# Hybrid diffusion step on one core: the adaLN sums of a feed-forward stage go behind its opening border, and each norm's reciprocal root takes one GpSimd step instead of two

## The chip, the cores and the metric

One Trainium2 chip, one core. The metric is the device time of one launch in microseconds; lower is better. Engines are called by the profile's names: PE (TensorE), DVE (VectorE), ACT (ScalarE), POOL (GpSimd) and SP (SyncE, which only issues transfers here).

## The reference, cut to what matters

Two layers of a hybrid backbone work on 128 context tokens and 256 latent tokens of width 1024, that is on three tiles of 128 tokens (t = 0 and 1 latent, t = 2 context). Each layer is a SwiGLU feed-forward step, a token mixing step and a second feed-forward step. Around each of them stands a norm, with shift, scale and gate from the conditioning vector (adaLN):

```python
def rms_norm(x, g):
    y = x * lax.rsqrt(jnp.mean(x * x, axis=-1, keepdims=True) + EPS)
    return y * g

m = jax.nn.silu(cond) @ p["w_ada"][l] + p["b_ada"][l]      # shift, scale, gate of 3 sub-layers
def pre(y, i):  return rms_norm(y, p["norm_pre"][l, i]) * (1.0 + scale[:, :, i]) + shift[:, :, i]
def post(y, i): return gate[:, :, i] * rms_norm(y, p["norm_post"][l, i])

x = x + 0.5 * post(swiglu(pre(x, 0), ...), 0)
x = x + post(token_mix(pre(x, 1), ...), 1)
x = x + 0.5 * post(swiglu(pre(x, 2), ...), 2)
```

Inside the mixing step there are further norms over heads of 64 (queries and keys of one attention group, the output of the other) and a layer norm.

## The kernel before

Weights stream in as 128x1024 fp32 pieces (`st`, queued on SP) and each is split into a rounded part and a remainder: ACT casts the first half of the tile `wu` (L167), DVE subtracts for the second (L168). Activations are split the same way (`split_pair`, L478 on ACT and L479 on DVE), and every product is three matmuls on PE (L556 to L558, L562 to L564, L590 to L592).

The stages run in the order ffn(0,0), mix(0), ffn(0,2), ffn(1,0), mix(1), ffn(1,2). Each ends in `rows_out`, the output product `ps_o`, whose last part runs token tile by token tile; behind the last matmul of a tile stand `post` (the sum of squares on ACT, `yg` on DVE, the reciprocal root on POOL, the new `x` on DVE) and `pre` of the next stage (squares of `x`, reciprocal root, `xn` on DVE, eight transposes `ps_t` on PE, `hf` on DVE and ACT, the split `h` on ACT and DVE). So there are five borders between stages: B1 (ffn(0,0) to mix(0)), B2 (mix(0) to ffn(0,2)), B3 (ffn(0,2) to ffn(1,0)), B4 (ffn(1,0) to mix(1)) and B5 (mix(1) to ffn(1,2)). At a border PE works on `ps_o` of the remaining tiles and then on the first projections of the next stage, `ps_j` in a mixing stage (24 matmuls of 512 columns for a token tile) and `ps_gu` in a feed-forward stage (also 24 for a tile), tile by tile.

A reciprocal root takes two steps on POOL: `ms` adds the two half sums and EPS (L489), `rstd` raises to the power -0.5 (L493). Inside the mixing stages L470 and L474 do the same for the head norms and the layer norm.

The adaLN vectors of coming sub-layers are summed inside the feed-forward stages: `Ada.step` multiplies a 128x1024 piece of `w_ada` (`ast`, queued on SP among the `st`) into two accumulators `acc` on DVE (L284 for the first piece, L288 for the others), and PE adds up the partitions when all eight are in (`ps_ada`, L300). The function `more` calls it a few times for every group of output columns.

The kernel's text is not in the order in which the engines work. A scheduler goes over the whole program, and by its own estimate of durations it decides for each engine the order of its queue; the engines then work through their queues in that order, and each instruction waits for its inputs by semaphores.

Of the kernel before, what the change touches and what calls it, by code (L numbers as in the profile page):

```python
# [2 lines left out]

# [1 line left out]

# [22 lines left out]
EPS = 1e-6  # L28
# [158 lines left out]
def kernel(ctx: ExitStack, tc: tile.TileContext, a: dict):  # L187
    nc = tc.nc
    PS = bass.MemoryType.PSUM

    cp = ctx.enter_context(tc.tile_pool(name="cp", bufs=1))
# [6 lines left out]
    sm = ctx.enter_context(tc.tile_pool(name="sm", bufs=4))  # L198
# [24 lines left out]
    x = []  # L223
    for t in range(NT):
        xt = xp.tile([P, D], F32, name=f"x{t}")
        src = a["x_sample"][0, t * P : (t + 1) * P, :] if t < 2 else a["x_prompt"][0]
        x.append((xt, src))

    mhalf = cp.tile([P, 8], F32, name="mhalf")
    nc.gpsimd.memset(mhalf, -0.5)  # L230
    ones = cp.tile([P, 32], F32, name="ones")
    nc.gpsimd.memset(ones, 1.0)
    sink = cp.tile([P, D], BF16, name="sink")
# [5 lines left out]
        out=sc,  # L239
        in_=scol.rearrange("p (i k) -> p k i", i=2).unsqueeze(2).to_broadcast([P, KC, 16, 2]),  # L240
# [148 lines left out]
    x = [t for t, _ in x]  # L389
# [75 lines left out]
            )  # L465


    def rstd_of(ss, n, width):
        ms = sm.tile([P, 8], F32, tag="ms", name=nm("ms"))
        nc.gpsimd.tensor_scalar(  # L470
            out=ms[:, 0:n], in0=ss, scalar1=1.0 / width, scalar2=EPS, op0=ALU.mult, op1=ALU.add
        )
        r = sm.tile([P, 8], F32, tag="rstd", name=nm("rstd"))
        nc.gpsimd.tensor_tensor(out=r[:, 0:n], in0=ms[:, 0:n], in1=mhalf[:, 0:n], op=ALU.pow)  # L474
        return r

    def split_pair(dst, sl, src):
        nc.scalar.copy(out=dst[:, 0, :, sl], in_=src)  # L478
        nc.vector.tensor_tensor(  # L479
            out=dst[:, 1, :, sl], in0=src, in1=dst[:, 0, :, sl].bitcast(F32), op=ALU.subtract  # L480
        )

    def new_pairs(s):
        return [hp.tile([P, 2, 2, TOK], F32R, tag="hc", name=nm(s)) for _ in range(4)]

    def rstd_two(ss):

        ms = sm.tile([P, 8], F32, tag="ms", name=nm("ms"))
        nc.gpsimd.tensor_scalar(  # L489
            out=ms[:, 0:1], in0=ss[:, 0:1], scalar1=ss[:, 1:2], scalar2=EPS, op0=ALU.add, op1=ALU.add  # L490
        )
        r = sm.tile([P, 8], F32, tag="rstd", name=nm("rstd"))
        nc.gpsimd.tensor_tensor(out=r[:, 0:1], in0=ms[:, 0:1], in1=mhalf[:, 0:1], op=ALU.pow)  # L493
        return r

    def pre_norm(t, xn):
        ss = sm.tile([P, 2], F32, tag="ss", name=nm("ss"))
        for hf in range(2):
            hsl = slice(hf * 512, (hf + 1) * 512)
            nc.scalar.activation(  # L500
                out=sink[:, hsl], in_=x[t][:, hsl], func=AF.Square, scale=D ** -0.5,
                accum_out=ss[:, hf : hf + 1],
            )
        r = rstd_two(ss)
        nc.vector.tensor_scalar(out=xn, in0=x[t], scalar1=r[:, 0:1], scalar2=None, op0=ALU.mult)

    def pre_half(l, i, t, hT, xn, half):
        A, B = mods[(l, i)][half]
        cond = 1 if t == 2 else 0
        sl = slice(t * P, (t + 1) * P)  # L510
        pt = mbank(nm("ps_t"))
        hf = tp.tile([P, 4, P], F32, tag="t2k", name=nm("hf"), bufs=4)
        for q in range(4):
            k = 4 * half + q
            nc.tensor.transpose(pt[:, q * P : (q + 1) * P], xn[:, k * P : (k + 1) * P], ident)
        for q in range(4):
            src = pt[:, q * P : (q + 1) * P]
            sa, sb = A[:, q, cond : cond + 1], B[:, q, cond : cond + 1]
            if q < MOD_DVE[half]:
                nc.vector.tensor_scalar(  # L520
                    out=hf[:, q, :], in0=src, scalar1=sa, scalar2=sb, op0=ALU.mult, op1=ALU.add
                )
            else:
                nc.scalar.activation(out=hf[:, q, :], in_=src, func=AF.Identity, scale=sa, bias=sb)
        for pr in range(2):
            split_pair(hT[2 * half + pr], sl, hf[:, 2 * pr : 2 * pr + 2, :])

    def pre(l, i, t, hT):
        xn = tp.tile([P, D], F32, tag="t4k", name=nm("xn"))
# [4 lines left out]
    def post(l, i, t, y):  # L534
        cond = 1 if t == 2 else 0
        G = gates[(l, i)][cond]
        ss = sm.tile([P, 2], F32, tag="ss", name=nm("ss"))
        yg = tp.tile([P, D], F32, tag="t4k", name=nm("yg"))
        for hf in range(2):
            hsl = slice(hf * 512, (hf + 1) * 512)  # L540
            nc.scalar.activation(
                out=sink[:, hsl], in_=y[hf], func=AF.Square, scale=D ** -0.5, accum_out=ss[:, hf : hf + 1]
            )
            nc.vector.tensor_tensor(out=yg[:, hsl], in0=y[hf], in1=G[:, hsl], op=ALU.mult)
        r = rstd_two(ss)
# [71 lines left out]
    def ffn(l, i, h, adas, nxt, first=None):  # L617
# [27 lines left out]
        with tc.tile_pool(name=nm("fp"), bufs=1) as fp:  # L645
# [3 lines left out]
            for t in range(NT):  # L649
# [71 lines left out]
    def mix(l, h, nxt):  # L721
        with tc.tile_pool(name=nm("mp"), bufs=1) as mp:
# [108 lines left out]
            def d_rows(t, ps):  # L831
# [3 lines left out]
                if t == 2:  # L835
# [4 lines left out]
                nc.vector.tensor_reduce(  # L840
                    out=ss[:, 0:6], in_=sq[:, 0:384].rearrange("p (h d) -> p h d", h=6), axis=AX.X, op=ALU.add
                )
                r = rstd_of(ss[:, 0:6], 6, 64)
                dn = mp.tile([P, 512], F32, tag="qk", name=nm("dn"), bufs=2)
                dv = dn[:, 0:384].rearrange("p (h d) -> p h d", h=6)
                nc.vector.tensor_tensor(
# [3 lines left out]
                    op=ALU.mult,  # L850
# [115 lines left out]
            def diff_unit(t, hd, box):  # L966
# [28 lines left out]
                def third():  # L995
# [129 lines left out]
            def norm_fill(t):  # L1125
# [172 lines left out]
```

## Time and profile before

| | before |
|---|---|
| device time, median of 3 runs | 1543.93 us (1543.18 to 1545.84) |
| the profiled execution: its time, its span | 1548.72 us, 1546.9 us |
| PE busy | 1492.0 us, 96% of the span |
| DVE busy | 1048.2 us, 68% |
| ACT busy | 635.4 us, 41% |
| POOL busy | 131.4 us, 8% |
| granted PE clock, mean | 0.993 of full speed |
| HBM | 256.36 MB read, 167 GB/s |

Busy time is the time in which an engine has an instruction in work. PE is busy nearly all the time, so a change in the time has to show in PE's idle time or in its clock.

### The profile page before, as it was taken

The numbers are of one execution on the slowest core, as the hardware profiler recorded it, in microseconds if no ns is written. First come the engines' busy times: TensorE is split into PE (matmuls) and PEld (weight loads), VectorE is DVE, ScalarE is ACT, GpSimd is POOL, SyncE is SP. The second block draws the span as 40 slices with busy tenths as digits, with TensorE's granted clock in tenths as the row PEclk, the third lists the DMA queues.
The fourth block names the chain that finished last, engine by engine and source line by source line (L and its number), as shares of the span: only waits on it lengthen the run. The fifth ranks groups of instructions, "written<-read, shape, count | busy, mean of one in ns | idle before, by whom it ended". The sixth has DMA issues, their size and how long they took to land. (4 is left out here: it accounts for less than half of the span.)

```text
span 1546.9 us, 20700 instructions
## 1 busy us (share of the span) xinstructions
PE 1492.0 (96%) x7924; PEld 1312.3 (85%) x7924; DVE 1048.2 (68%) x1454; ACT 635.4 (41%) x1103; POOL 131.4 (8%) x234
## 2 busy tenths in 40 slices
PE   5999999999999999999999999999999999999997
PEld 3799997777887899998879999887778879999885
DVE  3688889768887846677694666984798785334432
ACT  3442333273575633333263332334545763323331
POOL 1101000021011201000021000001200120000000
PEclk9999999999999999999999999999999999999999
DMA  8678667732224646566655566773322345344431
GB/s 318 231 235 274 228 223 242 242 109 97 69 69 150 204 133 203 201 214 195 197 166 182 183 196 202 234 237 100 124 74 91 108 146 168 123 136 141 134 108 41
DMA packets 73619, 260.13 MB, mean 168 GB/s; under 512 B 9728, under 2 KB 9856, under 8 KB 73520
## 3 DMA queue, kind: packets, MB, share of 16 engines
q1 hardware_dynamic: 68112, 246.32, 48.8%
q0 software_dynamic: 4976, 11.70, 2.8%
q8 instruction: 62, 1.02, 0.3%
q10 hardware_dynamic: 432, 0.79, 0.1%
q14 instruction: 37, 0.30, 0.1%
HBM read 256.36 MB, written 2.41 MB: 167 GB/s over the span
## 5 line engine op out<-in xcount | busy, mean ns | idle before, releaser
L168 DVE TENSOR_TENSOR wu<-st,wu 128x1024 fp32r<-128x1024 f32 x322 | 390.6, 1218 | 258.9 <-ACT wu L167 258.3
L167 ACT CAST wu<-st 128x1024 fp32r<-128x1024 f32 x322 | 337.1, 1052 | 536.2 <-PE ps_f L564 266.4
L562 PE MATMUL ps_f<-h,wu 128*128 128x384 f32 x1248 | 419.0, 336 | 0.0
L564 PE MATMUL ps_f<-h,wu 128*128 128x384 f32 x1248 | 417.1, 334 | 0.0
L563 PE MATMUL ps_f<-h,wu 128*128 128x384 f32 x1248 | 417.1, 334 | 0.0
L288 DVE SCALAR_TENSOR_TENSOR acc<-ast,sc,acc 128x1024 f32<-128x1024 f32 x224 | 279.6, 1281 | 35.0 <-DMA ast<-w_ada 34.6
L562 PEld LDWEIGHTS ps_f<-h,wu 128*128 128x128 f32 x1248 | 234.2, 188 | 7.5 <-issue 7.5
L563 PEld LDWEIGHTS ps_f<-h,wu 128*128 128x128 f32 x1248 | 234.3, 188 | 0.0
L564 PEld LDWEIGHTS ps_f<-h,wu 128*128 128x128 f32 x1248 | 234.2, 188 | 0.0
L590 PE MATMUL ps_o<-wu,hid_s 128*128 128x512 f32 x528 | 207.7, 393 | 0.0
L592 PE MATMUL ps_o<-wu,hid_s 128*128 128x512 f32 x528 | 206.3, 391 | 0.0
L591 PE MATMUL ps_o<-wu,hid_s 128*128 128x512 f32 x528 | 206.2, 391 | 0.0
L590 PEld LDWEIGHTS ps_o<-wu,hid_s 128*128 128x128 f32 x528 | 99.5, 188 | 26.0 <-issue 5.0
L592 PEld LDWEIGHTS ps_o<-wu,hid_s 128*128 128x128 f32 x528 | 99.5, 188 | 21.0
L591 PEld LDWEIGHTS ps_o<-wu,hid_s 128*128 128x128 f32 x528 | 99.6, 189 | 20.3
L702 ACT ACTIVATE sg<-ps_f 128x384 f32<-128x384 f32 x78 | 38.0, 487 | 114.1 <-PE ps_f L564 111.0
L556 PE MATMUL ps_j<-wu,h 128*128 128x512 f32 (+1 forms) x192 | 72.8, 379 | 0.0
L558 PE MATMUL ps_j<-wu,h 128*128 128x512 f32 (+1 forms) x192 | 70.5, 367 | 1.1 <-DVE h L479 1.1
L703 DVE TENSOR_TENSOR hid<-sg,ps_f 128x384 f32<-128x384 f32 x78 | 42.9, 550 | 40.4 <-PE ps_f L564 40.3
L557 PE MATMUL ps_j<-wu,h 128*128 128x512 f32 (+1 forms) x192 | 69.8, 363 | 0.0
L825 DVE SCALAR_TENSOR_TENSOR cacc<-upad,late,cacc 128x399 f32<-128x399 f32 x120 | 69.3, 628 | 0.0
L331 POOL DMA_DIRECT2D gd<-grow x24 | 11.8, 497 | 660.3 <-DVE grow L323 660.3
(234 smaller groups left out, 1698.1 us busy)
## 6 DMA issues: line engine op xcount, KB each, us to landing
st<-ws SPq DMA_DIRECT2D x320, 512.0 KB, 4.3
ast<-w_ada SPq DMA_DIRECT2D x128, 512.0 KB, 4.4
a<-ada SPq DMA_DIRECT2D x16, 512.0 KB, 10.2
G<-gd POOLq DMA_DIRECT2D x12, 512.0 KB, 4.2
brow<-b_ada POOLq DMA_DIRECT2D x24, 64.0 KB, 6.7
prow<-norm_post POOLq DMA_DIRECT2D x24, 64.0 KB, 6.9
x<-x_sample SPq DMA_DIRECT2D x2, 512.0 KB, 5.6
x<-x_prompt SPq DMA_DIRECT2D x1, 512.0 KB, 10.6
```

Of the source, the lines that this page charges most:

```text
L167: nc.scalar.copy(out=u[:, 0, :], in_=x)
L168: nc.vector.tensor_tensor(out=u[:, 1, :], in0=x, in1=u[:, 0, :].bitcast(F32), op=ALU.subtract)
L288: nc.vector.scalar_tensor_tensor(out=self.acc[c], in0=w, scalar=s1, in1=self.acc[c], op0=ALU.mult, op1=ALU.add)
L556: nc.tensor.matmul(out, lhsT=hk(h, k, 0, tsl), rhs=wh, start=start, stop=False)
L557: nc.tensor.matmul(out, lhsT=hk(h, k, 0, tsl), rhs=wl, start=False, stop=False)
L558: nc.tensor.matmul(out, lhsT=hk(h, k, 1, tsl), rhs=wh, start=False, stop=stop)
L562: nc.tensor.matmul(out, lhsT=wh, rhs=hk(h, k, 0, sl), start=start, stop=False)
L563: nc.tensor.matmul(out, lhsT=wh, rhs=hk(h, k, 1, sl), start=False, stop=False)
L564: nc.tensor.matmul(out, lhsT=wl, rhs=hk(h, k, 0, sl), start=False, stop=stop)
L590: nc.tensor.matmul(out, lhsT=pr[:, 0, s, tsl], rhs=u[:, 0, hsl], start=(q == 0), stop=False)
L591: nc.tensor.matmul(out, lhsT=pr[:, 0, s, tsl], rhs=u[:, 1, hsl], start=False, stop=False)
L592: nc.tensor.matmul(out, lhsT=pr[:, 1, s, tsl], rhs=u[:, 0, hsl], start=False, stop=(q == n - 1))
```

## The change

Three edits. First, `split_pair` returns its DVE instruction, `pre_half` keeps the last one in `border[0]`, and in a feed-forward stage every `Ada.step` is issued behind it: the scheduler has to queue each `acc` of the stage behind the last split of the border that opens the stage. (For ffn(0,0) there is no such border, and `edge` is None.) Second, the sums of squares of `post` and `pre`: each `Square` is followed on ACT by an `Identity` on 128x1 that adds EPS to the first half sum and, for the second half, the first result; POOL keeps only the power. Third, `ms` of the norms inside the mixing stage moves from POOL to DVE (`guarded`).

```diff
-    def rstd_of(ss, n, width):
+    def rstd_of(ms, n):
+        r = sm.tile([P, 8], F32, tag="rstd", name=nm("rstd"))
+        nc.gpsimd.tensor_tensor(out=r[:, 0:n], in0=ms, in1=mhalf[:, 0:n], op=ALU.pow)
+        return r
+
+    def guarded(ss, n, width):
         ms = sm.tile([P, 8], F32, tag="ms", name=nm("ms"))
-        nc.gpsimd.tensor_scalar(
+        nc.vector.tensor_scalar(
             out=ms[:, 0:n], in0=ss, scalar1=1.0 / width, scalar2=EPS, op0=ALU.mult, op1=ALU.add
         )
...
+        return rstd_of(ms[:, 0:n], n)
+
+    def half_square(half, src, ss):
+
+        nc.scalar.activation(
+            out=sink[:, 0:512], in_=src, func=AF.Square, scale=D ** -0.5, accum_out=ss[:, half : half + 1]
+        )
+        nc.scalar.activation(
+            out=ss[:, 2 + half : 3 + half], in_=ss[:, half : half + 1], func=AF.Identity,
+            bias=(ss[:, 2:3] if half else guard),
+        )
+
+    border = [None]
 
     def split_pair(dst, sl, src):
         nc.scalar.copy(out=dst[:, 0, :, sl], in_=src)
-        nc.vector.tensor_tensor(
+        return nc.vector.tensor_tensor(
...
-    def rstd_two(ss):
-
-        ms = sm.tile([P, 8], F32, tag="ms", name=nm("ms"))
-        nc.gpsimd.tensor_scalar(
-            out=ms[:, 0:1], in0=ss[:, 0:1], scalar1=ss[:, 1:2], scalar2=EPS, op0=ALU.add, op1=ALU.add
-        )
...
     def pre_norm(t, xn):
...
+            half_square(hf, x[t][:, hf * 512 : (hf + 1) * 512], ss)
+        r = rstd_of(ss[:, 3:4], 1)
...
-            split_pair(hT[2 * half + pr], sl, hf[:, 2 * pr : 2 * pr + 2, :])
+            border[0] = split_pair(hT[2 * half + pr], sl, hf[:, 2 * pr : 2 * pr + 2, :]).ins
...
             done, turns = [], []
+            edge = border[0]
...
-                    last = f.step(fp)
+                    with tc.issue_after(edge) if edge is not None else nullcontext():
+                        last = f.step(fp)
...
-                r = rstd_of(ss[:, 0:6], 6, 64)
+                r = guarded(ss[:, 0:6], 6, 64)
```

(`post` calls `half_square` in place of its `Square` as `pre_norm` does; the three norms of the mixing stage call `guarded`.)

All of this moves instructions in the queues, also where nothing was edited. Three places follow, with the rows of before first and those of the changed kernel second; line numbers of the changed kernel are 2 to 17 higher.

PE at B1, around the transposes of the second token tile. `ps_j_2843` and `ps_j_2845` are the projection of the first tile, `ps_j_2871` and `ps_j_2873` that of the second, `xn_2691` and `xn_2693` the second tile's normalised rows.

```order
L557 MATMUL ps_j_2843<-wu_2823,h_2561 128x512
L515 MATMUL ps_t_2700<-early,xn_2691 128x128 x4
L515 MATMUL ps_t_2714<-early,xn_2691 128x128 x4
L558 MATMUL ps_j_2843<-wu_2823,h_2561 128x512
L556 MATMUL ps_j_2843<-wu_2823,h_2561 128x512
L557 MATMUL ps_j_2843<-wu_2823,h_2561 128x512
...
L558 MATMUL ps_j_2843<-wu_2828,h_2562 128x512
L556 MATMUL ps_j_2871<-wu_2531,h_2559 128x512
```

```order
L558 MATMUL ps_j_2845<-wu_2830,h_2564 128x512
L559 MATMUL ps_j_2845<-wu_2830,h_2564 128x512
L518 MATMUL ps_t_2702<-early,xn_2693 128x128 x4
L518 MATMUL ps_t_2716<-early,xn_2693 128x128 x4
L557 MATMUL ps_j_2873<-wu_2533,h_2561 128x512
L558 MATMUL ps_j_2873<-wu_2533,h_2561 128x512
```

Before, 14 of the first tile's 24 matmuls stand ahead of the second tile's transposes and 10 behind them. Now all 24 stand ahead, and right behind the transposes comes a matmul that needs their result. The same has happened at the other borders: at B2, B3 and B5 the first tile had 6 or 7 of its 24 `ps_gu` ahead of those transposes and now has 24; ahead of the third tile's transposes stand now 24 `ps_j` of the second tile (before 15) at B1 and B4, and 42 `ps_gu` (before 29) at the others.

DVE at B1, second tile: `yg`, the new `x`, weight remainders `wu`, and `xn`.

```order
L544 TENSOR_TENSOR yg_2680<-ps_o_1987,G_1980 128x512
L548 SCALAR_TENSOR_TENSOR x_91<-yg_2680,rstd_2687,x_91 128x512 x2
L168 TENSOR_TENSOR wu_2823<-st_2478,wu_2823 128x1024
L168 TENSOR_TENSOR wu_2828<-st_2501,wu_2828 128x1024
L505 TENSOR_SCALAR xn_2691<-x_91,rstd_2697 128x1024
L544 TENSOR_TENSOR yg_2753<-ps_o_1988,G_1982 128x512
L544 TENSOR_TENSOR yg_2753<-ps_o_1989,G_1982 128x512
L520 TENSOR_SCALAR hf_2701<-ps_t_2700,A_1833,B_1834 128x128 x2
```

```order
L545 TENSOR_TENSOR yg_2682<-ps_o_1989,G_1982 128x512
L168 TENSOR_TENSOR wu_2825<-st_2480,wu_2825 128x1024
L168 TENSOR_TENSOR wu_2830<-st_2503,wu_2830 128x1024
L549 SCALAR_TENSOR_TENSOR x_91<-yg_2682,rstd_2689,x_91 128x512 x2
L168 TENSOR_TENSOR wu_2835<-st_2536,wu_2835 128x1024
L168 TENSOR_TENSOR wu_2840<-st_2559,wu_2840 128x1024
L508 TENSOR_SCALAR xn_2693<-x_91,rstd_2699 128x1024
L545 TENSOR_TENSOR yg_2755<-ps_o_1990,G_1984 128x512
L545 TENSOR_TENSOR yg_2755<-ps_o_1991,G_1984 128x512
L523 TENSOR_SCALAR hf_2703<-ps_t_2702,A_1835,B_1836 128x128 x2
```

Two `wu` now stand ahead of `x` that stood behind it, and two more have come in between `x` and `xn`; `x` and `xn` themselves are as before.

DVE at the opening of B2, first tile: `acc` are adaLN sums, `ast` their pieces of `w_ada`.

```order
L288 SCALAR_TENSOR_TENSOR acc_4650<-ast_4730,sc,acc_4650 128x1024
L544 TENSOR_TENSOR yg_4333<-ps_o_4202,G_4197 128x512
L548 SCALAR_TENSOR_TENSOR x_90<-yg_4333,rstd_4340,x_90 128x512 x2
L288 SCALAR_TENSOR_TENSOR acc_4651<-ast_4730,sc,acc_4651 128x1024
L505 TENSOR_SCALAR xn_4344<-x_90,rstd_4350 128x1024
L544 TENSOR_TENSOR yg_4406<-ps_o_4203,G_4197 128x512
L288 SCALAR_TENSOR_TENSOR acc_4650<-ast_4799,sc,acc_4650 128x1024
```

```order
L545 TENSOR_TENSOR yg_4335<-ps_o_4203,G_4199 128x512
L545 TENSOR_TENSOR yg_4335<-ps_o_4204,G_4199 128x512
L549 SCALAR_TENSOR_TENSOR x_90<-yg_4335,rstd_4342,x_90 128x512 x2
L508 TENSOR_SCALAR xn_4346<-x_90,rstd_4352 128x1024
L545 TENSOR_TENSOR yg_4408<-ps_o_4205,G_4199 128x512
L523 TENSOR_SCALAR hf_4356<-ps_t_4355,A_2572,B_2573 128x128 x2
```

The three `acc` of these rows have gone, and so have those that stood ahead of and behind them; they come now behind the last split `h` of the third tile. In the same way they have left B3 and B5.

## Rows read from the trace of the kernel before

**Rows 1.** The waits of PE over the whole span: what PE waited for, us in total, times, the longest in us.

```profile
PE ps_t L515 <- DVE xn L505: 14.9, 14, 2.7
PE ps_dT L873 <- DVE dr L757: 3.4, 2, 1.7
```

**Rows 2.** The timeline of PE at the first border (B1), from 316 to 341 us: start in us, duration in us, engine, line, operation, tiles, shape, count, and in brackets the idle time before it and what ended it.

```profile
317.68 1.06 PE L515 MATMUL ps_t<-early,xn 128*128 128x128 f32 x8 [1.28 <-DVE xn L505]
318.50 0.47 PE L590 MATMUL ps_o<-wu,hid_s 128*128 128x512 f32 x1
318.82 0.39 PE L591 MATMUL ps_o<-wu,hid_s 128*128 128x512 f32 x1
319.05 0.40 PE L592 MATMUL ps_o<-wu,hid_s 128*128 128x512 f32 x1
...
329.13 1.09 PE L515 MATMUL ps_t<-early,xn 128*128 128x128 f32 x8 [1.05 <-DVE xn L505]
...
333.76 0.50 PE L558 MATMUL ps_j<-wu,h 128*128 128x512 f32 x1 [0.56 <-DVE h L479]
...
337.51 1.09 PE L515 MATMUL ps_t<-early,xn 128*128 128x128 f32 x8 [0.50 <-DVE xn L505]
```

**Rows 3.** The waits of PE again, of one border each: first B4 (1061 to 1100 us, two rows), then B2 (496 to 526 us, three), B3 (783 to 814 us, three) and B5 (1248 to 1279 us, its first row; its other two read as those of B2).

```profile
PE ps_t L515 <- DVE xn L505: 2.8, 3, 1.3
PE ps_j L558 <- DVE h L479: 0.6, 1, 0.6
...
PE ps_t L515 <- DVE xn L505: 3.8, 3, 2.7
PE ps_gu L557 <- DVE wu L168: 0.6, 1, 0.6
PE ps_gu L556 <- ACT h L478: 0.3, 1, 0.3
...
PE ps_t L515 <- DVE xn L505: 2.6, 2, 2.0
PE ps_gu L556 <- ACT h L478: 0.6, 1, 0.6
PE ps_gu L557 <- DVE wu L168: 0.2, 1, 0.2
...
PE ps_t L515 <- DVE xn L505: 2.8, 3, 1.7
```

**Rows 4.** The timeline of DVE around the second token tile of B1 (columns as in Rows 2).

```profile
322.82 0.69 DVE L544 TENSOR_TENSOR yg<-ps_o,G 128x512 f32<-128x512 f32 x1
323.87 1.42 DVE L548 SCALAR_TENSOR_TENSOR x<-yg,rstd,x 128x512 f32<-128x512 f32 x2 [0.36 <-POOL rstd L493]
325.21 2.35 DVE L168 TENSOR_TENSOR wu<-st,wu 128x1024 fp32r<-128x1024 f32 x2
328.32 0.75 DVE L505 TENSOR_SCALAR xn<-x,rstd 128x1024 f32<-128x1024 f32 x1 [0.77 <-POOL rstd L493]
```

**Rows 5.** The timeline of ACT at B1: the first tile (two rows), the second (one), the third (one).

```profile
318.79 1.51 ACT L524 ACTIVATE hf<-ps_t,B,A 128x128 f32<-128x128 f32 x4 [2.51 <-PE ps_t L515]
320.17 0.72 ACT L478 CAST h<-hf 128x256 fp32r<-128x256 f32 x2
...
322.91 2.01 ACT L167 CAST wu<-st 128x1024 fp32r<-128x1024 f32 x2
...
334.94 1.28 ACT L806 ACT_TABLE_LOAD   x1
```

**Rows 6.** The timeline of POOL at B1, second tile.

```profile
326.26 1.38 POOL L489 TENSOR_SCALAR ms<-ss 128x1 f32<-128x1 f32 x1 [1.83 <-ACT sink L500]
327.73 0.56 POOL L493 TENSOR_TENSOR rstd<-ms,mhalf 128x1 f32<-128x1 f32 x1
```

**Rows 7.** The timeline at the other borders: DVE and POOL at B2, then POOL at B3 and at B5.

```profile
491.00 1.28 DVE L288 SCALAR_TENSOR_TENSOR acc<-ast,sc,acc 128x1024 f32<-128x1024 f32 x1 [2.06 <-DMA ast<-w_ada]
...
490.19 0.57 POOL L493 TENSOR_TENSOR rstd<-ms,mhalf 128x1 f32<-128x1 f32 x1
...
777.56 1.82 POOL L489 TENSOR_SCALAR ms<-ss 128x1 f32<-128x1 f32 x1 [9.79 <-ACT sink L541]
...
1243.64 1.53 POOL L493 TENSOR_TENSOR rstd<-ms,mhalf 128x1 f32<-128x1 f32 x1
```

**Rows 8.** Groups of instructions by line with shapes kept apart: busy us, mean ns of one | idle time before them and what ended it.

```profile
L452 ACT ACTIVATE lam<-lam 128x4 f32<-128x4 f32 x1 | 0.2, 207 | 3.4 <-DVE lam L451 3.4
L524 ACT ACTIVATE hf<-ps_t,B,A 128x128 f32<-128x128 f32 x90 | 35.4, 463 | 23.5 <-PE ps_t L515 23.2
L489 POOL TENSOR_SCALAR ms<-ss 128x1 f32<-128x1 f32 x36 | 23.7, 658 | 255.1 <-ACT sink L541 191.7 <-ACT sink L500 62.8
L470 POOL TENSOR_SCALAR ms<-ss 128x6 f32<-128x6 f32 x6 | 4.2, 708 | 50.9 <-DVE ss L840 50.9
L168 DVE TENSOR_TENSOR wu<-st,wu 128x1024 fp32r<-128x1024 f32 x320 | 389.3, 1222 | 258.9 <-ACT wu L167 258.3
```

**Rows 9.** Busy time by engine, 785.7 to 789.0 us, just behind the first transposes of B3: start and end, us, then busy us of each engine (instructions); the third figure from the end is the granted clock as a share of full speed.

```profile
785.70:789.00 3.30, 3.30 (x10) 2.52 (x9) 3.30 (x8) 3.24 (x11) 0.62 (x1) 0.50 0.02 5
```

**Rows 10.** The start: timeline of PE from 0 to 20 us.

```profile
14.12 2.27 PE L404 MATMUL ps_first<-a,sc 128*32 128x256 f32 x16 [14.12 <-DMA a<-ada]
...
19.27 0.38 PE L1236 MATMUL ps_t<-early,xn 128*128 128x128 f32 x2
```

More of the change, by code (lines that the diff above doesn't have):

```diff
@@ L1 @@
 import math
-from contextlib import ExitStack
+from contextlib import ExitStack, nullcontext
 import numpy as np
@@ L230 @@
     nc.gpsimd.memset(mhalf, -0.5)
+    guard = cp.tile([P, 1], F32, name="guard")
+    nc.gpsimd.memset(guard, EPS)
     ones = cp.tile([P, 32], F32, name="ones")
@@ L465, in lam_setup @@
             )
-    def rstd_of(ss, n, width):
+    def rstd_of(ms, n):
[3 more added lines that the diff above has]
+    def guarded(ss, n, width):
         ms = sm.tile([P, 8], F32, tag="ms", name=nm("ms"))
-        nc.gpsimd.tensor_scalar(
+        nc.vector.tensor_scalar(
             out=ms[:, 0:n], in0=ss, scalar1=1.0 / width, scalar2=EPS, op0=ALU.mult, op1=ALU.add
         )
-        r = sm.tile([P, 8], F32, tag="rstd", name=nm("rstd"))
-        nc.gpsimd.tensor_tensor(out=r[:, 0:n], in0=ms[:, 0:n], in1=mhalf[:, 0:n], op=ALU.pow)
-        return r
+        return rstd_of(ms[:, 0:n], n)
[8 more added lines that the diff above has]
+    border = [None]
     def split_pair(dst, sl, src):
         nc.scalar.copy(out=dst[:, 0, :, sl], in_=src)
-        nc.vector.tensor_tensor(
+        return nc.vector.tensor_tensor(
             out=dst[:, 1, :, sl], in0=src, in1=dst[:, 0, :, sl].bitcast(F32), op=ALU.subtract
@@ L484, in new_pairs @@
         return [hp.tile([P, 2, 2, TOK], F32R, tag="hc", name=nm(s)) for _ in range(4)]
-    def rstd_two(ss):
-        ms = sm.tile([P, 8], F32, tag="ms", name=nm("ms"))
-        nc.gpsimd.tensor_scalar(
-            out=ms[:, 0:1], in0=ss[:, 0:1], scalar1=ss[:, 1:2], scalar2=EPS, op0=ALU.add, op1=ALU.add
-        )
-        r = sm.tile([P, 8], F32, tag="rstd", name=nm("rstd"))
-        nc.gpsimd.tensor_tensor(out=r[:, 0:1], in0=ms[:, 0:1], in1=mhalf[:, 0:1], op=ALU.pow)
-        return r
     def pre_norm(t, xn):
-        ss = sm.tile([P, 2], F32, tag="ss", name=nm("ss"))
+        ss = sm.tile([P, 4], F32, tag="ss", name=nm("ss"))
         for hf in range(2):
[L499 to L504, printed above, removed]
+            half_square(hf, x[t][:, hf * 512 : (hf + 1) * 512], ss)
+        r = rstd_of(ss[:, 3:4], 1)
         nc.vector.tensor_scalar(out=xn, in0=x[t], scalar1=r[:, 0:1], scalar2=None, op0=ALU.mult)
@@ L536, in post @@
         G = gates[(l, i)][cond]
-        ss = sm.tile([P, 2], F32, tag="ss", name=nm("ss"))
+        ss = sm.tile([P, 4], F32, tag="ss", name=nm("ss"))
         yg = tp.tile([P, D], F32, tag="t4k", name=nm("yg"))
@@ L540, in post @@
             hsl = slice(hf * 512, (hf + 1) * 512)
-            nc.scalar.activation(
-                out=sink[:, hsl], in_=y[hf], func=AF.Square, scale=D ** -0.5, accum_out=ss[:, hf : hf + 1]
-            )
+            half_square(hf, y[hf], ss)
             nc.vector.tensor_tensor(out=yg[:, hsl], in0=y[hf], in1=G[:, hsl], op=ALU.mult)
-        r = rstd_two(ss)
+        r = rstd_of(ss[:, 3:4], 1)
         for hf in range(2):
@@ L1015, in third @@
                     )
-                    rb = rstd_of(ss[:, 0:4], 4, 64)
+                    rb = guarded(ss[:, 0:4], 4, 64)
                     nc.vector.tensor_tensor(
@@ L1135, in norm_fill @@
                 nc.vector.bn_aggr(out=mv_, in_=st)
-                r = rstd_of(mv_[:, 1:2], 1, 1.0)
+                r = guarded(mv_[:, 1:2], 1, 1.0)
                 z = mp.tile([P, 256], F32, tag="ctmp", name=nm("z"), bufs=2)
```

## The prediction, made before the changed kernel was run

> **What bounds the kernel now.** I read the list of PE's waits first. The table above has PE busy for 96% of the span, so only PE's waits, its clock and the ends of the run can move the time. The list says that PE waited 14 times for `xn`, 14.9 us in all, and twice for `dr` in the mixing stages, 3.4 us [rows 1]; the adaLN product `ps_ada` doesn't occur in it. Split by border [rows 2, 3], the waits of PE are 3.4 us at B1 (1.28 for the first tile's `xn`, 1.05 for the second's, 0.56 for a remainder of `h`, 0.50 for the third's `xn`), 3.4 at B4, 4.7 at B2, 3.4 at B3 and 3.7 at B5: 18.6 us together. The reader should see in [rows 2] that these waits are short because PE has matmuls of the tile before to do while a norm is being made.
>
> **The change, part by part.** *Power step.* A norm loses `ms` on POOL, which takes 0.29 to 0.31 us when nothing is in its way but 0.66 in the mean [rows 8], since POOL is held while DVE works on SBUF data: 1.38 us behind two `wu` that end at 327.56 [rows 4, 6], and 1.82 at B3 [rows 7]. It gains two `Identity` on ACT. The trace has none of 128x1; the bounds are 0.21 us (ACT on 128x4) and 0.46 (ACT on 128x128 with scale and bias from memory) [rows 8]. I take 0.21, the row nearest in size. The first overlaps with the second `Square` in `post`; per norm some 0.2 to 0.4 us are added and 0.4 (0.30, and 0.1 between the two POOL steps) are taken away, so an unheld chain gains 0.1 or nothing. The power step can still be held, and then `ms` going saves nothing, since the power step waits in its place (`rstd` took 1.53 at B5 [rows 7]).
>
> The Trainium skill ("ScalarE: Activation LUTs", section "What ACT_TABLE_LOAD costs") gives about 0.28 us to an ACTIVATE whose bias is a 128x1 pointer, which both new ones have; no row here shows such a one of 128x1. By it about five Identities on each border's path would cost 0.07 more each, an estimate of some 2 us more over five borders.
>
> *adaLN sums.* At B2 an `acc` stood ahead of `yg` and `x` and waited 2.06 us for its `ast`, though the root it kept from use was ready at 490.76 [rows 7]. That goes, and so do the `acc` in B3 (they held `ms` for 1.82) and B5. Behind the border they cost nothing: PE never waits for `ps_ada`, and DVE is idle for 258.9 us ahead of its 322 `wu`, 0.8 us each, waiting for ACT's cast [rows 8]. If that cover were gone, each `acc` of 1.28 us [rows 7] would delay a `wu`. On SP the `ast` move behind `st` that are issued well ahead, and on POOL the issue of a gate's load (`G`) goes ahead of B1's second power step, which is held at that time anyway; no cost from either. ffn(0,0) has no edge and keeps its order.
>
> *The order.* This is the large part. In B1, where `acc` play no role, I follow the second tile in the clock of [rows 2, 4, 5]. `yg` ends at 323.51. Two `wu` now come next; they follow the casts from 322.91 on, 1.0 us each, with an `Identity` between, and end at about 326.3 (2.35 for the pair). The power step, ready at 324.2, is held by them, and is out about 0.45 later, at 326.75. `x` then starts 2.9 us later than the traced 323.87. Its squares and Identities end at 329.4; two more `wu` (from 328.1 to 330.45) hold the next power step; `xn` runs from 330.9 to 331.65, and PE's transposes can start at 331.7 instead of 329.13. PE gets there later as well, by the 10 matmuls moved ahead, 0.228 us each (the starts at 318.82 and 319.05 in [rows 2]) or 2.28: it waits 1.05 + 2.57 - 2.28 = 1.35. Taking all queues start by start, with the power step held across the gap between two `wu`, I get 1.8. I take 1.6.
>
> Then comes what before had cover. From PE's last transpose to the first `h` it is about 2.2 us: transposes from 317.68, PE free at 318.50, `hf` on ACT to 320.2, first cast of `h` done near 320.6 [rows 2, 5]. Those 10 matmuls (2.3 us) lay in it; now none does, and PE waits the 2.2 us, instead of 0.56. At B2, B3 and B5 a fifth `hf` stands ahead of the casts (0.35), so 2.5.
>
> The third tile: at B1 its second `Identity` stands behind a table load (1.28 [rows 5]), the sigmoid and all casts of `h`; `xn` comes late by 1.3 instead of 0.50, and behind its transposes 9 matmuls of cover are gone, so 1.8 of bare waiting. At B2, B3 and B5 six `ps_gu` are left (1.4 us of cover): 0.4 for `xn` and 0.8 behind.
>
> The first tile's wait comes out at 1.2 everywhere (traced 1.28, 2.67, 2.03, 1.66 [rows 2, 7 and 3]): without `acc` all borders open alike.
>
> **The sum.** B1 and B4: 1.2 + 1.6 + 2.2 + 1.3 + 1.8 = 8.1. B2, B3 and B5: 1.2 + 1.6 + 2.5 + 0.4 + 0.8 = 6.5. Done the same way for the kernel before, the working gives 4.6 at B1 and B4, 5.75 at B2, 5.7 at B3 and 4.75 at B5, which is 1.0 to 1.2 above the traced waits (2.3 at B3, where the clock was down and swallowed waiting), because it places transposes a little too close. So like is set against like: 2 x 3.5 + 0.75 + 0.8 + 1.75 = +10.3 us. Set against the traced 18.6 it would be 35.7 - 18.6 = +17; that is the upper end.
>
> The start gives nothing: PE waits for a transfer until 14.12 and needs `xn` only at 19.27, without a wait [rows 10]. In the mixing stages `ms` on DVE saves at most the 0.71 us it took on POOL [rows 8], with the next conv step possibly holding the power step for as much; PE's wait there is 1.7 [rows 1]. I put 0, with -0.7 to +0.6 per layer as bounds. The last norms save about 0.2.
>
> On the profiled execution, 1548.72 us with a span of 1546.9, this gives 1558.8. That execution is 4.8 us (0.3%) above the median of the runs, which have no profiler; carried to the median of 1543.93 it is about **1554.1 us**, 0.7% slower. From no change a measurement of this kernel can tell about 0.2%, 3.1 us.
>
> **Rivals.** *Roots come early enough, and it is faster.* Place: the second tile. If the power step isn't held by the `wu` ahead of `x`, and DVE's `wu` come out sooner, `xn` is there when PE arrives; the point from which it decides is `xn` of B1's second tile ready 1.6 us sooner than I step it, near 330.4. Then the sum falls to 2 x 6.5 + 3 x 4.9 = 27.7 against 25.4, +2.3. If the first tile's wait then shrinks from 1.2 to 0.4, as both its chains lose `ms` unheld, 4 us more go, and 0.7 in each mixing stage: -3.1, 1540.8 us; a little more and it is clearly faster. For it: `ms` lost 36 x 0.36 = 13 us to being held [rows 8]. Against: DVE's queue runs in order, and the `wu` stand ahead of `x` whatever POOL does; the bare wait for `h` stays in any case.
>
> *The parts cancel.* The first half of that rival alone: `xn` not late, +2.3, 1546.2 us, within 0.2%.
>
> *The clock falls at each border.* Once in the middle of the run it did: behind the first transposes of B3, after 2.0 us of waiting, the granted clock was 0.50, that is 1.2 GHz, for 3.3 us [rows 3, 9]; behind B2's 2.67 us it wasn't. My stepped borders have 1.6 us of waiting, transposes, and 2.2 to 2.5 of waiting. At half clock 3.3 us of matmuls lose 1.65, of which later waits gave back about 0.7 at B3. Four more of these cost 4 to 6.6 us: 1558 to 1561 us.
>
> **Chances.** My forecast, 1548 to 1558: 0.52. Clock: 0.2. Cancel: 0.13. Faster side: 0.15. So slower by over 0.2% (above 1547.0) 0.72, within 0.2% 0.13, faster (below 1540.8) 0.15. The range that leaves out two in ten runs from the cancelling case to the top of the clock's, 1542 to 1562; the forecast's own is 1548 to 1558.
>
> **What would show it.** In the changed kernel: PE's waits for `xn` still near 1.2 at each border's first tile, with no `acc` there; a new wait of 2 to 2.5 us for `h` (released by ACT) right behind the second tile's transposes at all five borders; `wu` between `yg` and `xn` on DVE with `rstd` held beside them; about 30 us of waits at borders. Wrong I am if the wait for the second tile's `xn` is gone, if the waits for `h` are under 1 us, or if the time went into the feed-forward bodies (a `wu` late behind `acc`), where I expect no waits.

## The result, and the profile after

The changed kernel takes **1560.2 us** (median of 4 runs, 1557.94 to 1562.13); 1554.1 was predicted, with 1548 to 1558 as the forecast's own range and 1542 to 1562 as the wide one. The median lies 16.3 us above the 1543.93 of the kernel before; the ratio of the two kernels' runs was measured as 1.0088 [1.0064, 1.0112], and in a second comparison, side by side (1560.51 against 1545.89 us), as 1.0094 [1.0080, 1.0109]. So it is some 14 to 16 us slower, where +10.2 was forecast.

The page of the changed kernel, its first line and that of busy times:

```profile
span 1560.4 us, 20768 instructions
PE 1500.1 (96%) x7924; PEld 1319.4 (85%) x7924; DVE 1051.6 (67%) x1472; ACT 656.6 (42%) x1175; POOL 106.3 (7%) x181
```

The span grew by 13.5 us. PE has the same 7924 instructions and is busy 8.1 us longer (1500.1 against 1492.0), so part of the loss is not waiting. Its idle time grew by the other 5.4 us.

The waits of PE over the whole span (what it waited for, us in total, times, the longest):

```profile
PE ps_t L518 <- DVE xn L508: 12.6, 12, 1.4
...
PE ps_gu L557 <- ACT h L495: 8.8, 7, 2.2
PE ps_j L557 <- ACT h L495: 3.8, 2, 1.9
PE ps_dT L876 <- DVE dr L760: 3.6, 2, 1.8
PE ps_uT L797 <- ACT hf L527: 3.2, 2, 1.6
```

The wait for `xn` has become smaller (12 waits, 14 in [rows 1]). The wait of `ps_gu` for `h` from ACT has grown to 8.8 us, from 1.7 in four waits of at most 0.6 before, and two groups are new: `ps_j` behind the same `h`, 3.8 us, and `uT` behind ACT's `hf`, 3.2. The timeline of PE at B1, where [rows 2] showed four short waits, tells where they are (columns as there):

```profile
316.10 1.06 PE L518 MATMUL ps_t<-early,xn 128*128 128x128 f32 x8 [1.17 <-DVE xn L508]
...
329.39 1.09 PE L518 MATMUL ps_t<-early,xn 128*128 128x128 f32 x8 [0.86 <-DVE xn L508]
332.37 0.80 PE L557 MATMUL ps_j<-wu,h 128*128 128x512 f32 x1 [1.89 <-ACT h L495]
332.96 0.63 PE L558 MATMUL ps_j<-wu,h 128*128 128x512 f32 x1
333.39 0.63 PE L559 MATMUL ps_j<-wu,h 128*128 128x512 f32 x1
...
335.45 0.39 PE L558 MATMUL ps_j<-wu,h 128*128 128x512 f32 x1
335.68 0.40 PE L559 MATMUL ps_j<-wu,h 128*128 128x512 f32 x1
...
339.35 1.04 PE L518 MATMUL ps_t<-early,xn 128*128 128x128 f32 x8
341.99 0.44 PE L797 MATMUL ps_uT<-early,u 128*128 128x128 f32 x2 [1.60 <-ACT hf L527]
```

All 24 matmuls of the first tile now stand ahead of the second tile's transposes, so behind those PE has nothing: 1.89 us of bare waiting (0.56 before), and 1.60 behind the third tile's. The starts tell the second thing. At 332.96 and 333.39 matmuls start 0.43 apart, from 335.45 on 0.23, which is the distance in [rows 2]. The busy times of that stretch, and of one at B4 (columns as in [rows 9], the third figure from the end is the granted clock), say why:

```profile
331.90:335.30 3.40, 2.93 (x7) 2.36 (x8) 1.95 (x5) 2.23 (x8) 0.57 (x1) 0.50 0.40 161
1099.90:1103.30 3.40, 2.80 (x8) 2.31 (x9) 1.52 (x4) 2.73 (x9) 0.00 (x0) 0.50 0.00 0
```

PE's clock had fallen to its lower level, 1.2 GHz, just there. In this execution it fell at four borders: behind the second tile's transposes at B1, B2 and B5 (3.4, 6.8 and 6.8 us), and at B4 behind the third tile's (the second row). At B3, with waits of the same length, it didn't. It fell twice inside the second mixing stage as well (6.8 us from 1130.6 and 3.4 from 1178.4), at no border. Without the one at the end of the run, which both kernels have, all stretches together are 30.7 us, against 13.7 in the trace of before; at borders they are 20.5 against 3.4, and elsewhere 10.2 in both. Half of the 17 us more at the borders is 8.5, about what PE's busy time grew by.

By border, PE's waits are 5.5 us at B1, 5.3 at B2, 5.1 at B3, 6.7 at B4 and 5.3 at B5, 27.8 together against 18.6: +9.2. In return PE began at 12.00 us instead of 14.12 [rows 10] because its first transfer came sooner (in the profiles of all later runs, the kernels without an Identity among them, it came at 12.2 to 12.9, so the 14.12 looks like that of one execution), and 1.7 us of smaller waits went, 1.4 of it the waits for `p` in the mixing stages (0.92 and 0.94 before, 0.5 together now). 9.2 - 2.1 - 1.7 = 5.4.

The second tile on DVE and POOL (B1), against [rows 4, 6]:

```profile
321.24 0.69 DVE L545 TENSOR_TENSOR yg<-ps_o,G 128x512 f32<-128x512 f32 x1
322.18 2.36 DVE L168 TENSOR_TENSOR wu<-st,wu 128x1024 fp32r<-128x1024 f32 x2 [0.25 <-ACT wu L167]
324.46 1.41 DVE L549 SCALAR_TENSOR_TENSOR x<-yg,rstd,x 128x512 f32<-128x512 f32 x2
325.78 2.36 DVE L168 TENSOR_TENSOR wu<-st,wu 128x1024 fp32r<-128x1024 f32 x2
328.58 0.75 DVE L508 TENSOR_SCALAR xn<-x,rstd 128x1024 f32<-128x1024 f32 x1 [0.44 <-POOL rstd L472]
```

```profile
322.83 1.00 POOL L472 TENSOR_TENSOR rstd<-ss,mhalf 128x1 f32<-128x1 f32 x1
327.38 1.16 POOL L472 TENSOR_TENSOR rstd<-ss,mhalf 128x1 f32<-128x1 f32 x1 [3.56 <-ACT ss L487]
```

Two `wu` now stand between `yg` and `x`, and two between `x` and `xn`. POOL's power step takes 1.00 and 1.16 us beside them (0.56 in [rows 6]); it is held as `ms` was. On ACT, the third tile's second `Identity` has been put behind a table load, the sigmoid, `hf` and the casts of `h`:

```profile
328.73 1.28 ACT L809 ACT_TABLE_LOAD   x1
330.03 0.38 ACT L809 ACTIVATE u<-ps_j 128x256 f32<-128x256 f32 x1
330.52 1.50 ACT L527 ACTIVATE hf<-ps_t,B,A 128x128 f32<-128x128 f32 x4
331.91 0.72 ACT L495 CAST h<-hf 128x256 fp32r<-128x256 f32 x2
...
333.80 0.32 ACT L487 ACTIVATE ss<-ss 128x1 f32<-128x1 f32 x1
```

The squares it adds up ended at 328.71; its sum comes out at 334.1.

### The profile page after: what moved, and what is told of

Same layout as the page of the kernel before. It is cut to its first block, busy times and chain, and to the rows that moved or that the text cites. A ratio compares the mean times of both kernels' runs of the same rounds, so it can differ in the third digit from the quotient of the medians.

```text
span 1560.4 us, 20768 instructions
## 1 busy us (share of the span) xinstructions
PE 1500.1 (96%) x7924; PEld 1319.4 (85%) x7924; DVE 1051.6 (67%) x1472; ACT 656.6 (42%) x1175; POOL 106.3 (7%) x181
## 5 line engine op out<-in xcount | busy, mean ns | idle before, releaser
L557 PE MATMUL ps_j<-wu,h 128*128 128x512 f32 (+1 forms) x192 | 74.5, 388 | 3.8 <-ACT h L495 3.8
L559 PE MATMUL ps_j<-wu,h 128*128 128x512 f32 (+1 forms) x192 | 71.6, 373 | 0.0
L558 PE MATMUL ps_j<-wu,h 128*128 128x512 f32 (+1 forms) x192 | 71.4, 372 | 0.0
L557 PE MATMUL ps_gu<-wu,h 128*128 128x512 f32 x120 | 51.5, 429 | 8.8 <-ACT h L495 8.8
```

What stands on the lines that cost most here:

```text
L557: nc.tensor.matmul(out, lhsT=hk(h, k, 0, tsl), rhs=wh, start=start, stop=False)
L558: nc.tensor.matmul(out, lhsT=hk(h, k, 0, tsl), rhs=wl, start=False, stop=False)
L559: nc.tensor.matmul(out, lhsT=hk(h, k, 1, tsl), rhs=wh, start=False, stop=stop)
```

## The experiments

Two questions were open: which of the three edits costs the time, and whether it is the Identities themselves (work added to each norm) or the order of the queues that the scheduler makes of them; then, how much of the loss is PE's clock. A first set takes the edits apart. In all diffs the lines not shown are those of the kernel before, or of the changed kernel where it says so.

**The edge alone.** `Ada.step` behind the border, nothing else:

```diff
+            edge = border[0]
...
-                    last = f.step(fp)
+                    with tc.issue_after(edge) if edge is not None else nullcontext():
+                        last = f.step(fp)
```

> The kernel before with the first edit alone: adaLN sums queued behind the opening border of their feed-forward stage; both POOL steps of every root stay, and no Identity. Theory A (the loss comes from the queue order that the Identities bring, with the edge as bystander): all borders keep 10 matmuls of the first tile behind the second tile's transposes, so no wait of 2 us for h; the waits at B2, B3 and B5 come near the 3.4 us of B1, and the time is 1539 to 1544 us. Rival B (the edge itself moves the work: acc pile up behind the border and delay weights): 1550 us or more, with new waits in the feed-forward bodies or at B2, B3, B5.

Measured: 1544.63 us, just above the forecast 1539 to 1544; ratio 0.9986 [0.9976, 0.9996]. The timeline of PE at B2, its rows with a wait:

```profile
492.83 1.09 PE L517 MATMUL ps_t<-early,xn 128*128 128x128 f32 x8 [1.20 <-DVE xn L507]
504.31 1.09 PE L517 MATMUL ps_t<-early,xn 128*128 128x128 f32 x8 [1.06 <-DVE xn L507]
508.94 0.50 PE L560 MATMUL ps_gu<-wu,h 128*128 128x512 f32 x1 [0.56 <-DVE h L481]
512.68 1.09 PE L517 MATMUL ps_t<-early,xn 128*128 128x128 f32 x8 [0.50 <-DVE xn L507]
```

The 2.67 us of the first tile [rows 3] are 1.20, and all five borders read like B1 before, 3.3 us each. All five borders have the order of B1 now, 14 of the first tile's matmuls ahead of the second tile's transposes. So the edge is a small gain.

**The Identities alone.** The sums of `post` and `pre` as in the changed kernel, no edge, `ms` of the mixing stage on POOL:

```diff
+        nc.scalar.activation(
+            out=ss[:, 2 + half : 3 + half], in_=ss[:, half : half + 1], func=AF.Identity,
+            bias=(ss[:, 2:3] if half else guard),
+        )
...
-            edge = border[0]
+            edge = None
```

> The second edit alone: each Square of post and pre is followed by an Identity on ACT and POOL keeps only the power step; adaLN sums as before (no edge), ms of the mixing stage's norms stays on POOL. Theory A: the order at B1 and B4 is that of the changed kernel, so waits of 1.9 us for h and 1.6 us behind the third tile there, granted clock down beside them; 1554 to 1566 us, most of the loss or all of it. Rival B: the Identities only lengthen chains by 0.1 us or so each, 1543 to 1547 us.

Measured: 1568.37 us, above the forecast 1554 to 1566; ratio 1.0145 [1.0130, 1.0159]. Its waits of PE at B2:

```profile
PE ps_gu L557 <- ACT h L495: 3.8, 2, 2.2
PE ps_t L518 <- DVE xn L508: 2.3, 1, 2.3
PE ps_gu L559 <- DVE h L496: 0.4, 1, 0.4
```

6.5 us at B2, with two bare waits for `h` (1.54 and 2.24), the second at a place where the changed kernel has only 0.50. The whole loss is in this edit, and more than the whole: the two other edits, which gain 0.2% between them without the Identities (next experiment), take 0.5 to 0.6% off it. How the two share in that no run shows.

**`ms` of the mixing norms on DVE alone**, and then **the edge with it**, without the Identities:

```diff
-        nc.gpsimd.tensor_scalar(
+        nc.vector.tensor_scalar(
             out=ms[:, 0:n], in0=ss, scalar1=1.0 / width, scalar2=EPS, op0=ALU.mult, op1=ALU.add
```

> The third edit alone: ms of the 18 norms inside the mixing stages on DVE in place of POOL. Theory A: 1542 to 1545 us, PE's wait for dr (1.7 us, twice) as before within 0.3. Rival C (the power step of a head norm is now held by the conv step behind ms): the wait for dr grows by 0.5 us or more in each mixing stage and the time by 1 to 3 us, 1545 to 1547.

> First and third edit together, without the Identities (both POOL steps in the norms at the borders). Theory A: 1539 to 1544 us, at or a little below the kernel with the edge alone; the changed kernel's 1560 would then be the Identities' doing by 16 us or more. Rival B: 1550 us or more.

Measured: 1543.72 us, 0.9983 [0.9972, 0.9993], and 1542.78 us, 0.9982 [0.9970, 0.9994]. `dr` comes 0.1 us later in each mixing stage (1.79 against 1.69), but a wait of 0.92 us for `p` at 462.59 in the kernel before is gone. The two together, that is the change without its second edit, beat the kernel before by 0.2%. The ratio of the two together isn't lower than that of either alone by more than the measurement can tell.

**All three edits, with the queues as before.** The changed kernel's arithmetic, instruction for instruction; but edges that bind only the order put the border's instructions into the sequence that the kernel before has at B1, and the edge alone at all five borders (14 of the first tile's matmuls ahead of the second tile's transposes, `wu` behind `x`, the table load behind the third tile's sums). Of the edges, three:

```diff
+                if open_ and t < 2 and 3 * k + j >= 14 + t:
+                    edge = mark['pt', t + 1]
...
+                with tc.issue_after(mark['act', 2]) if t == 0 else nullcontext():
+                    nc.scalar.activation(out=u, in_=ps[:, 0:256], func=AF.Sigmoid)
...
+                with tc.issue_after(mark['hf', 1]) if nxt and t == 2 else nullcontext():
+                    mark['x', t] = nc.vector.scalar_tensor_tensor(
```

> The changed kernel with all three edits, but with the order of the queues at the borders tied to that of the kernel before by order-only edges: 10 matmuls of the first tile behind the second tile's transposes on PE, x ahead of the two wu on DVE, each second Identity right behind its Square on ACT. Theory A (the order costs, the Identities themselves nearly nothing): no wait of 2 us for h, border waits of 3 to 5 us each, 1541 to 1549 us. Rival E (the Identities lengthen each chain so much that order is secondary): waits for xn of 2 us and more at each border, 1553 us or more.

Measured: 1542.27 us, ratio 0.9979 [0.9967, 0.9990]. Its waits of PE at B1:

```profile
PE ps_t L524 <- DVE xn L514: 3.0, 3, 1.2
PE ps_j L598 <- ACT h L501: 0.3, 1, 0.3
PE ps_j L598 <- DVE h L502: 0.2, 1, 0.2
```

3.5 us, as before the change (3.4). With 72 Identities in it, this kernel is as fast as the one without them. So it is the order and not the Identities' own time that costs the 0.9%; this was shown by an edit that changes nothing but the order. That edit undoes all the moves at once, so how the cost divides among PE's, DVE's and ACT's queues isn't shown.

**The changed kernel with the bare waits filled.** Useless matmuls (9 behind the second tile's transposes, 7 or 2 behind the third's) into a bank that the next product starts afresh:

```diff
+        for k in range(pad):
+            u = units[0].rearrange("p s (k n) -> p s k n", k=KC // len(units))
+            with tc.issue_after(mark['pt', t]):
+                nc.tensor.matmul(out, lhsT=hk(h, k % 2, 0, slice(0, P)), rhs=u[:, 0, k % 2, :], start=True, stop=True)
```

> The changed kernel with matmuls without use put into the bare waits: 9 of 512 columns right behind the second tile's transposes at each border, 7 (B1, B4) or 2 (B2, B3, B5) behind the third tile's; their results are overwritten. They take up waiting time and nothing else. Theory F (a good part of the loss is the granted clock, which falls beside these waits): the stretches of half clock at B1, B2, B4 and B5 go, and the time falls by 4 to 9 us, to 1551 to 1556 us, although more work is done. Rival G (the waits alone are the loss, the clock a bystander): 1558 to 1563 us as for the changed kernel.

Measured: 1553.49 us, ratio 1.0049 [1.0032, 1.0066]. The changed kernel had not been timed beside it, so both were run side by side:

> The changed kernel once more, beside the next kernel on the same chip. Both theories: ratio to the kernel before 1.006 to 1.011, granted clock over the span about 0.988.

> The changed kernel with useless matmuls in the bare waits for h (its outputs don't change), beside the changed kernel in the same call. Theory (some 40% of the loss is the granted clock, which falls where the second tile's transposes stand between two waits): 0.3 to 0.5% below the changed kernel, with the granted clock over the span 0.993 or higher. Rival (the clock has no part in it, chips differ): the same as the changed kernel within 0.2%.

Measured: 1560.51 us (1.0094 [1.0080, 1.0109]) and 1556.42 us (1.0061 [1.0043, 1.0079]): 0.33% less with 65 matmuls more. Stretches around the five borders, first of the changed kernel (B1 to B5 in order; start and end, then busy us of PE, PEld, DVE, ACT and POOL with their instructions; the third figure from the end is the mean granted clock):

```profile
317.00:345.00 28.00, 23.36 (x106) 18.71 (x107) 18.09 (x33) 22.09 (x58) 4.58 (x9) 0.94 0.33 113
496.00:530.00 34.00, 29.87 (x132) 24.09 (x131) 23.14 (x41) 25.12 (x62) 6.51 (x9) 0.90 0.28 90
786.00:822.00 36.00, 32.40 (x148) 26.64 (x149) 25.40 (x44) 26.07 (x63) 6.25 (x10) 0.91 0.39 129
1078.00:1108.00 30.00, 25.38 (x114) 20.38 (x115) 19.32 (x36) 23.83 (x61) 4.58 (x9) 0.94 0.32 106
1256.00:1290.00 34.00, 29.76 (x131) 23.98 (x132) 22.86 (x40) 24.87 (x62) 5.50 (x7) 0.90 0.23 75
```

then of the same kernel with the waits filled:

```profile
317.00:345.00 28.00, 26.07 (x124) 20.76 (x123) 17.99 (x33) 23.48 (x60) 4.58 (x9) 1.00 0.36 114
496.00:530.00 34.00, 31.07 (x149) 24.56 (x148) 23.71 (x42) 26.57 (x68) 6.18 (x8) 1.00 0.25 80
786.00:822.00 36.00, 33.80 (x166) 27.84 (x167) 27.46 (x46) 26.44 (x65) 7.47 (x12) 1.00 0.40 137
1077.00:1107.00 30.00, 28.00 (x134) 22.55 (x135) 19.63 (x35) 24.39 (x61) 4.57 (x9) 1.00 0.30 107
1256.00:1290.00 34.00, 32.20 (x157) 26.20 (x158) 25.17 (x44) 25.17 (x63) 7.99 (x12) 1.00 0.30 95
```

At all five borders the clock fell without the filling, and at none with it. The expected 0.3 to 0.5% were met at their lower end. The granted clock of the span was 0.991 and not 0.993: in that execution it fell at the start (19.2 to 26.1) and in the mixing stages instead (370.8 to 377.6, 418.6 to 422.0, 1132.0 to 1135.4 us). Where it didn't, the gain is larger: the 13 runs of the filled kernel took 1550.7 to 1553.5 us where their granted clock was 0.996 or more, and 1554.9 to 1559.2 where it was 0.991 to 0.993; the changed kernel's eight, at 0.987 to 0.989, took 1557.9 to 1562.1. So the clock is worth 4 to 5 us (4.1 by the medians, 0.33% by the ratios) and about 8 where it stays up.

**Smaller doses of the same edit** (diffs against the changed kernel). First the changed kernel with one Identity for a norm instead of two (EPS is left out), then with none, the sum and EPS in one DVE step:

```diff
-        nc.scalar.activation(
-            out=ss[:, 2 + half : 3 + half], in_=ss[:, half : half + 1], func=AF.Identity,
-            bias=(ss[:, 2:3] if half else guard),
-        )
+        if half == 1:
+            nc.scalar.activation(
+                out=ss[:, 3:4], in_=ss[:, 1:2], func=AF.Identity, bias=ss[:, 0:1]
+            )
```

> The changed kernel with one Identity a norm instead of two: the second adds the first half sum directly, and EPS is left out of these norms. The scheduler then puts 24 and 18 ps_j of the first two tiles ahead of the next transposes at B1 and B4 (24 and 24 with two Identities), and 21 or 24 and 15 to 17 ps_gu at the others. Theory A: waits behind the second tile's transposes of 1.3 to 2.2 us (3 or no matmuls of cover), less waiting behind the third tile's (6 matmuls of cover at B1 and B4); 1550 to 1558 us, between before and changed. If only the length of the chain mattered, half the loss would go: about 1552; if order alone mattered at B2 and B5 3 matmuls would give back 0.7 us each.

```diff
+        if half == 1:
+            nc.vector.tensor_scalar(
+                out=ss[:, 3:4], in0=ss[:, 0:1], scalar1=ss[:, 1:2], scalar2=EPS, op0=ALU.add, op1=ALU.add
+            )
```

> Changed kernel, but the sum of a norm's two halves and EPS is one DVE step behind the second Square; no Identity is left in the norms' sums, POOL still has only the power step. The first tile's matmuls ahead of the second tile's transposes are then 21 (14 in the kernel before, 24 in the changed one), and 15 to 22 ahead of the third's. Theory (the order of the queues costs the time, not the Identities): the waits for h behind the second tile's transposes stay, near 1.2 us at B1 and B4 (3 matmuls more of cover, 0.7 us off 1.9); ratio to the kernel before 1.002 to 1.006. Rival (the Identities themselves lengthen the chains): with none of them and one POOL step less than before, at or below 1.000, as with the edge alone (0.9986).

Measured: 1553.3 us, 1.0048 [1.0035, 1.0060], and 1549.44 us, 1.0030 [1.0018, 1.0042]. The time of the first doesn't tell the two theories apart (1550 to 1558 and about 1552). Its trace does at B2, where 21 and not 24 of the first tile's matmuls stand ahead of the transposes: the wait for `h` is 1.54 us, 0.70 shorter than the 2.24 of the changed kernel, which is what three matmuls of cover were to give back; but a wait of 0.57 for the remainder of `h` has come behind it. In the second the waits of PE at B1 are:

```profile
PE ps_j L557 <- ACT h L495: 1.5, 1, 1.5
PE ps_t L518 <- DVE xn L508: 1.5, 2, 0.9
PE ps_j L559 <- DVE h L496: 0.7, 1, 0.7
PE ps_uT L797 <- ACT hf L527: 0.5, 1, 0.5
```

Without an Identity and with one POOL step less than before, it is still slower: 21 of the first tile's matmuls stand ahead of the second tile's transposes, and the waits for `h` are there at all five borders. Part of its loss is something else, one wait of 2.0 us for `ps_ada` in ffn(0,0). The rival that blames the Identities' time forecast 1.000 or less, and is out. The wait for `h` came out longer than the 1.2 us I gave it: 1.54, and 0.68 for its remainder. Five `hf` stand ahead of the first cast of `h` there (1.86 us), as at B2, and not four (1.50).

Side by side (matmuls at B1 by the program, first those of the first tile ahead of the second tile's transposes, then those between the second and the third tile's, with the useless ones behind a plus sign; the wait for `h` behind the second tile's transposes by the trace; borders of five with the clock at half speed behind them in the profiled execution):

| kernel | matmuls | wait for `h` at B1, us | borders with half clock | ratio |
|---|---|---|---|---|
| before | 14, 25 | 0.56 | 1 | 1 |
| edge alone | 14, 25 | 0.56 | 0 | 0.9986 |
| all three, old order | 14, 25 | 0.28 + 0.22 | 0 | 0.9979 |
| sum on DVE | 21, 22 | 1.54 + 0.68 | 3 | 1.0030 |
| one Identity | 24, 18 | 1.89 | 4 | 1.0048 |
| changed, waits filled | 24, 24 + 9 | none | 0, 0 | 1.0049, 1.0061 |
| changed | 24, 24 | 1.89 | 4, 5 | 1.0088, 1.0094 |
| Identities alone | 24, 24 | 1.89 | 5 | 1.0145 |

## Why the prediction was right, and where it was short

*The order, second tile.* Right in kind, a little too dear. In the clock of the changed trace B1 lies 1.6 us earlier. I had `x` 2.9 us later than in [rows 4]; it is 2.2 later (324.46 + 1.58 = 326.04 against 323.87), since the power step was out before the second `wu` ended. `xn` starts at 328.58 where I had 329.3. The wait is 0.85 to 0.86 at B1, B3 and B4 and 1.39 at B2 and B5; I took 1.6.

*Bare wait for `h`.* 1.89 at B1 and B4, 2.24 at the others; 2.2 and 2.5 were worked out from the transposes and `hf` of [rows 2, 5]. It is new, it stands at all five borders, and ACT releases it: the main step was right.

*Third tile.* I had 1.3 and 1.8 at B1 and B4. It is 0 and 1.60 at B1, 1.10 and 1.60 at B4. The 0 at B1 is no better `xn`: PE ran at half clock from 331.9 to 335.3 and came late itself; with the waits filled and the clock up, the same wait is 1.07. At B2, B3 and B5 0.4 and 0.8 were forecast, 0 to 0.28 and 0.50 to 0.52 measured.

*First tile.* 1.13 to 1.23 at all five borders, forecast 1.2. The edge alone gives 1.20 to 1.28 there, so the `acc` were what stood in front of B2, B3 and B5. How much they cost varies: with `ms` on DVE alone, where the `acc` are still there, the waits at these three are 1.36, 2.03 and 1.41; at B2 an `acc` waited 0.87 us for its `ast` there and not 2.06.

*The sum of waits.* +9.2 measured, +10.3 forecast. Setting like against like, with the same arithmetic done for the kernel before, was what kept this right; against the traced 18.6 it would have been +17. The match owes something to errors that cancel: by level I had 35.7 us for the changed kernel, 7.9 above the 27.8 measured, and 25.4 for the kernel before, 6.8 above the 18.6. And the sum held only the waits at borders. Outside it, 3.8 us of other waits went (2.1 at the start, 1.7 smaller ones) and 8.1 us of busy time came.

*The clock: the step that failed.* I kept the clock out of the sum and gave it to a rival, four borders more at half clock and 4 to 6.6 us, 1558 to 1561 us in all, at a chance of 0.2. That rival is what happened, and the 1560.2 us lie in its range and above the forecast's own. PE's busy time grew by 8.1 us, the clock stood at half speed behind four and five borders of two executions, and filling the bare waits gave 4 to 5 us back. The trace of before had shown such a fall once, at B3: a wait of 2.03 us ahead of the transposes, and then a granted clock of 0.50 [rows 3, 9]. I set B2 against it, where the clock hadn't fallen behind 2.67. That let me pass over what my own steps had produced five times and the kernel before had at no border: a wait, transposes, and a second wait of 2 us.

*Power step and Identities.* I took 0.21 us for an Identity by [rows 8]. The groups of ACT in the changed kernel (busy us, mean ns):

```profile
L487 ACT ACTIVATE ss<-ss 128x1 f32<-128x1 f32 x36 | 10.7, 297 | 0.9
L487 ACT ACTIVATE ss<-ss,guard 128x1 f32<-128x1 f32 x36 | 10.6, 295 | 1.4 <-ACT sink L484 0.2
```

It is 0.30. The Trainium skill's figure for an ACTIVATE with a pointer as bias ("ScalarE: Activation LUTs", section "What ACT_TABLE_LOAD costs"), about 0.28 us, was the nearer one. The estimated 2 us that hung on it don't show: with the old order, 72 of them cost nothing that can be measured.

*Mixing stages and adaLN sums.* I put 0 for `ms` on DVE, with -0.7 to +0.6 us for a layer; alone it gives 0.17% [0.07%, 0.28%], 1.1 to 4.3 us for the two layers, so 0 was too cautious. In its trace PE waits 1.4 us less for `p` and 0.2 more for `dr` in the two stages. The later `acc` cost nothing that shows in the feed-forward bodies: PE waits once for `ps_ada`, 0.3 us at 293.5, where it waited not at all before, and that is in ffn(0,0), which has no edge.

*The faster rival and the cancelling one* needed B1's second `xn` ready by 330.4. It was ready at 329.33 + 1.58 = 330.91, half a microsecond too late, and PE still waited 0.86 for it; the bare wait for `h` came on top in any case.

What stays open: why the scheduler moves ten matmuls forward for a step of 0.3 us. Its estimates were not read; the two smaller doses show only that it moves fewer for less.

## What to carry to other kernels

Where a scheduler orders the queues by its own estimates, the cost of an edit is not its instructions' time but the order that comes out: compare the queues of both programs first, and look for matmuls that have slid from behind a transpose (where they cover the next wait) to ahead of it. An edit that is good in itself can be kept by binding the old order with edges; here this turns +0.9% into -0.2%. And where the new order puts a few transposes between two waits of PE, price the clock with it, not the waits alone.

## What the runs showed of the hardware that was not expected

The granted clock fell to 0.50, that is to 1.2 GHz, for 3.4 to 6.8 us at 21 of the 25 borders that had waits of 1.5 us or more for `h` behind their transposes (five executions: the Identities alone, the changed kernel twice, the two smaller doses), and at 2 of the 35 where such a wait was missing or filled (before, edge alone, `ms` on DVE alone, both, old order, and the filled kernel twice); those 2 are B3 in the first and the third of these, with a wait of 2.03 us for `xn`. PE was busy for most of these stretches (26.7 of 30.7 us in the changed kernel's first trace), so each costs about half its length, less what later waits give back. With matmuls whose results nobody reads in the waits, the clock stayed up at all ten borders of two executions, and the kernel with 65 more of them was the faster one.

Such a wait is not the whole story. In the same twelve traces the clock fell 11 times inside the mixing stages, six of them within 2 us behind PE's wait of 1.8 us for `dr` (which occurs 24 times), the other five with no wait of PE shown in the 20 us ahead. What decides between the borders and waits that bring it and those that don't isn't shown.
